# One quarter of the low parts on GpSimd, and a fourth seven-product chunk in three feed-forward parts

## The chip, the cores and the metric

The kernel runs on one core of a Trainium2 chip. The core has five engines with instruction queues of their own: TensorE (PE in the profile; its weight loads are shown as PEld), VectorE (DVE), ScalarE (ACT), GpSimd (POOL) and SyncE (SP), which only issues transfers. The metric is the device time of one launch, in microseconds (us); less is better.

## The reference

Two layers, each of them: half a feed-forward step, a mixer (self-attention of one of two kinds, and attention into a memory), half a feed-forward step. The sequence has 256 rows of 1024 values, all in 32-bit floats. A feed-forward part is

```
def swiglu(h, w_gate, w_up, w_down):          # (1024, 2816), (1024, 2816), (2816, 1024)
    return (jax.nn.silu(h @ w_gate) * (h @ w_up)) @ w_down
...
h = rmsnorm(x, ffn1_norm[i])
x = x + 0.5 * swiglu(h, ffn1_w_gate[i], ffn1_w_up[i], ffn1_w_down[i])
```

There are four such parts (two layers, two steps). They are called parts 1 to 4 here; in the code they are `(l, nm)` = (0, 1), (0, 2), (1, 1), (1, 2). The mixer of layer 1 stands between parts 3 and 4.

## The kernel before

**Split weights.** No product is a single matmul. A weight block `raw` (f32) is split into `hi`, its value rounded to fp32r by ScalarE (line 338, `split_hi`), and `lo` = `raw` - `hi`, made by VectorE (line 356, `split_lo`). The activations are split in the same way (`xh`, `xl`). Each product is then three matmuls of 512 columns into one PSUM tile: hi with xh (line 511), lo with xh (line 514), hi with xl (line 517), in `dense`.

**Chunks.** Weights come in chunks of 1 MB (128 partitions x 2048), loaded on SyncE's queue into three buffers `raw`. Each chunk has four units of 512 columns, q = 0 to 3. `hi` and `lo` have four buffers of 2048 columns each. In `dense`, TensorE waits for the low part of the unit that it needs, so all of a chunk's units are needed, but one after another. A raw buffer comes free when its splits are done, a hi and lo buffer when TensorE has used it.

**A feed-forward part.** The gate and up weights make 22 chunks (11 groups of 256 columns, two halves of the inner dimension). Eighteen are plain: two units at a time are split (`w` = 2, 1024 columns), and a chunk is used in 24 matmuls. The other four are multiplied by a scheme with seven products for eight (`pair_items`), for which VectorE forms sums of blocks (`wsum`, line 350) before they are split. The down weights make 11 chunks of 256 rows, c = 0 to 10. A plain one is split unit by unit (512 columns) and used in 24 matmuls. In parts 2 to 4 the chunks in `SEVEN`, 1, 4 and 7, are multiplied by the scheme with seven products: four sums (`wsum`), seven units to split instead of four (the last three of them in tiles called `gxh` and `gxl` for all but the first such chunk), 21 matmuls, and four sums of activation blocks (`sf`, line 681) with their own split (`h` from `hr`, lines 690 and 694) in the place of the one split of `ht` (lines 665 and 667). The last three down chunks are used together, 6 matmuls of each in turn.

**Order.** The program is written out engine by engine at build time. A planner, `Flow`, keeps an estimate of the time at which each engine will be free, and Python generators (`split_hi`, `split_lo`, `evac`, `finish`, ...) emit their next instruction when the estimate says that its inputs are there (`calm_v`: when VectorE is less than 0.4 us behind). On the chip each engine then works its own list strictly in order and waits where an input is late. The planner's estimates are not measured times, and do not know of one engine holding up another.

**GpSimd** before the change computes the rotary tables (between 120 and 200 us), reciprocal square roots by a power operation (`rsqrt`, line 532), and one of the two rotary products (line 1259).

Of the kernel before, what the change touches and what calls it, by code (L numbers as in the profile page):

```python
# [12 lines left out]
F32 = mybir.dt.float32  # L13
# [13 lines left out]
NG = FF // 256  # L27
# [15 lines left out]
SLACK = 0.4  # L43
# [99 lines left out]
def kernel(  # L143
# [10 lines left out]
    nc = tc.nc  # L154
    PSUM = bass.MemoryType.PSUM
    NRAW, NHL, NT2 = 3, 4, 19
    flow = Flow()
# [27 lines left out]
    def load_x(tb, hf, queue=None):  # L185
        (queue or nc.sync).dma_start(out=xs[tb][:, hf * 512:(hf + 1) * 512],
                                     in_=x[0, tb * P:(tb + 1) * P, hf * 512:(hf + 1) * 512])
# [53 lines left out]
    class Chunk:  # L241
        def __init__(self, parts):
            self.parts = parts
            self.raw = self.arrive = None
            self.block = [None] * 4

    class Item:
# [3 lines left out]
        def __init__(self, raws, uses=8, w=1):  # L251
            self.raws, self.uses = raws, uses
            self.hi = self.lo = None
            self.hit, self.lot, self.st = [None] * 7, [None] * 7, [None] * 4
            self.n, self.frees, self.takes, self.gives, self.guest = 1, 1, 0, 0, False
            self.sums, self.t = [], []
            self.index = len(items)
            w = 1 if len(items) < 2 else w
            self.units = [(self.own(q, w), q, w, None) for q in range(0, 4, w)]
            items.append(self)  # L260

        def own(self, q, w=1, i=0):
            return lambda: self.raws[i].raw[:, q * 512:(q + w) * 512]
# [7 lines left out]
    chunks, items = [], []  # L271
    raw_left = [NRAW]
# [6 lines left out]
    def add_raw(parts):  # L279
        chunks.append(Chunk(parts))  # L280
        return chunks[-1]

    def add_chunk(parts, uses=8, w=1):
        return Item([add_raw(parts)], uses, w)

    def loader():
        for i, c in enumerate(chunks):
            yield lambda: raw_left[0] > 0
            raw_left[0] -= 1
            c.raw = wraw.tile([P, 2048], F32, tag="raw", name=f"raw{i}")  # L290
            dma_free[0] = max(dma_free[0], flow.now)
            n = len(c.parts)
            for j, (dst, src) in enumerate(c.parts):
                nc.sync.dma_start(out=dst(c.raw), in_=src)
                dma_free[0] += 2.9 / n
                if i < 2 and j % 2:
                    for q in range((j - 1) * 4 // n, (j + 1) * 4 // n):
                        c.block[q] = dma_free[0] + LAT
                if i == 1 and j == 1:
                    load_x(1, 1)  # L300
                    dma_free[0] += 0.7
            c.arrive = dma_free[0] + LAT
            c.block = [t or c.arrive for t in c.block]
            if i == 0:
                load_x(0, 1)
                dma_free[0] += 0.7
            if i > 4 and late_done[0] < len(late_loads):
                dst, src = late_loads[late_done[0]]
                late_done[0] += 1
                nc.sync.dma_start(out=dst, in_=src)  # L310
                dma_free[0] += 0.3
# [4 lines left out]
    def calm_v(i):  # L316
        return lambda: flow.free["V"] <= flow.now + SLACK or i <= at[0] + AHEAD
# [24 lines left out]
    def split_lo():  # L342
        for i, it in enumerate(items):
            if it.sums:
                yield lambda: all(r.raw is not None for r in it.raws) and g2.left >= it.takes + 2
                yield max(r.arrive for r in it.raws)
                it.t += [g2.take([P, 512], F32, "wsum") for _ in range(it.takes)]
                for j, (x, y) in enumerate(it.sums):
                    yield calm_v(i)
                    nc.vector.tensor_sub(it.t[j], x(), y())  # L350
                    it.st[j] = flow.dve(512)
            for src, q, w, dep in it.units:
                yield lambda: it.hit[q] is not None
                yield it.hit[q]
                yield calm_v(i)
                nc.vector.tensor_sub(it.part(1, q, w), src(), it.part(0, q, w).bitcast(F32))  # L356
                t = flow.dve(512 * w)
                it.lot[q:q + w] = [t] * w
            raw_left[0] += it.frees
            g2.give(it.gives)  # L360

    def k4(t):
        return t.rearrange("p (k n) -> p k n", k=4)
# [4 lines left out]
    def cols4(w, c, c0, n, o, pieces=1):  # L368
        st = 4 // pieces
        return [((lambda raw, a=a: k4(raw)[:, a:a + st, o:o + n]),  # L370
                 w[c * 512 + a * P:c * 512 + (a + st) * P, c0:c0 + n].rearrange("(k p) n -> p k n", p=P))
                for a in range(0, 4, st)]
# [1 line left out]
    def rows2(w, r):  # L374
        return [(lambda raw: k2(raw), w[r * 256:(r + 1) * 256, :].rearrange("(k p) n -> p k n", p=P))]

    SEVEN = {(0, 1): (), (0, 2): (1, 4, 7), (1, 1): (1, 4, 7), (1, 2): (1, 4, 7)}
    PAIR = {(0, 1): 4, (0, 2): 3, (1, 1): 3, (1, 2): 3}

    def turned2(w, r):  # L380
        src = w[r * 256:(r + 1) * 256, :].rearrange("(k b i) n -> b i k n", k=2, b=4)
        return [((lambda raw, b=b: k2(raw)[b::4]), src[b]) for b in range(4)]
# [6 lines left out]
    def seven_item(it, guest):  # L389

        r = [it.own(q) for q in range(4)]
        t = lambda j: lambda: it.t[j]
        it.n, it.uses, it.takes, it.gives, it.guest = 1 if guest else 2, 7, 4, 4, guest
        it.sums = [(r[1], r[0]), (r[3], t(0)), (r[3], r[1]), (r[2], t(1))]
        it.units = [(r[0], 0, 1, None), (r[2], 1, 1, None), (r[3], 2, 1, None)] + [(t(j), 3 + j, 1, j) for j in range(4)]
# [46 lines left out]
    def plan_ffn(l, nm, wg, wu, wd):  # L442
        def parts(g, c):
            pieces = (4, 2)[len(chunks)] if len(chunks) < 2 else 1
            a = cols4(wg[l], c, g * 256, 256, 0, pieces)
            b = cols4(wu[l], c, g * 256, 256, 256, pieces)
            return [q for ab in zip(a, b) for q in ab]

        gu = {}
        pair = PAIR[l, nm]  # L450
        work = [(g, c) for g in range(NG) for c in range(2)]
        if pair is not None:
            rest = [w for w in work if w[0] not in (pair, pair + 1)]
            n = 2 * pair
            p = iter(rest[n:])
            work = rest[:n]
            loads = {}
            for x in ("11", "m1", "p", "12", "m5", "p", "22", "m7", "p", "m6", "p", "m3", "p", "p", "21", "m2", "p", "m4"):
                work.append(next(p) if x == "p" else x)
            work += list(p)  # L460
            blocks = {"11": (pair, 0), "12": (pair + 1, 0), "22": (pair + 1, 1), "21": (pair, 1)}
            raws = [Chunk(parts(*blocks[x])) for x in ("11", "12", "22", "21")]
            made, mk = pair_items(raws)
            which = dict(zip(("11", "12", "22", "21"), raws))
        for w in work:
            if w in ("11", "12", "22", "21"):
                chunks.append(which[w])
            elif isinstance(w, str):
                mk[w]()
            else:  # L470
                gu[w] = add_chunk(parts(*w), 8, 2)
        plan[l, nm, "gu"] = gu
        plan[l, nm, "work"] = [w for w in work if w not in ("11", "12", "22", "21")]
        if pair is not None:
            plan[l, nm, "pair"] = made
        dn = []
        for c in range(NG):
            dn.append(add_chunk(turned2(wd[l], c)))
            if c in SEVEN[l, nm]:
                seven_item(dn[-1], c != SEVEN[l, nm][0])  # L480
            elif c >= NG - 3:
                u = dn[-1].units
                u[1], u[2] = u[2], u[1]
        plan[l, nm, "dn"] = dn
# [133 lines left out]
    def ffn(l, nm, xt, gc_next):  # L618
        hts = [None] * NG
        htt = [None] * NG  # L620
        sv = SEVEN[l, nm]
        prog = [-1]
# [997 lines left out]
        return nxt  # L1620


    flow.spawn(loader(), idle=True)
    flow.spawn(split_hi(), idle=True)
    flow.spawn(split_lo(), idle=True)
    flow.step()
    xt = Xt(PAIR[0, 1] is not None)

# [90 lines left out]
```

## Time and profile before

| | |
|---|---|
| median of 3 runs | 955.98 us (955.21 to 956.04) |
| the profiled execution, its own time | 955.69 us |
| its span in the trace | 953.9 us |
| instructions | 13334 |
| TensorE, VectorE, ScalarE, GpSimd busy | 99%, 86%, 62%, 11% of the span |
| parts 2, 3, 4 in the trace | about 315 to 492, 492 to 668, 774 to 954 us |

A busy engine is one with an instruction in progress. Matmuls overlap in the trace: each is shown with 0.39 us, while the next one starts earlier. VectorE's instructions overlap a little too, so the price of one in a row of them is the distance between starts.

### The profile page before, as it was taken

The numbers are of one execution on the slowest core, as the hardware profiler recorded it, in microseconds if no ns is written. First come the engines' busy times: TensorE is split into PE (matmuls) and PEld (weight loads), VectorE is DVE, ScalarE is ACT, GpSimd is POOL, SyncE is SP. The second block draws the span as 40 slices with busy tenths as digits, with TensorE's granted clock in tenths as the row PEclk, the third lists the DMA queues.
The fourth block names the chain that finished last, engine by engine and source line by source line (L and its number), as shares of the span: only waits on it lengthen the run. The fifth ranks groups of instructions, "written<-read, shape, count | busy, mean of one in ns | idle before, by whom it ended". The sixth has DMA issues, their size and how long they took to land.

```text
span 953.9 us, 13334 instructions
## 1 busy us (share of the span) xinstructions
PE 945.6 (99%) x4475; PEld 774.1 (81%) x4475; DVE 820.0 (86%) x1483; ACT 587.0 (62%) x1121; POOL 109.1 (11%) x160
## 2 busy tenths in 40 slices
PE   9999999999999999999999999999999999999998
PEld 7888888887777888888888888888787778888886
DVE  7898978888777899979889899796999888999884
ACT  6556566677676746647546656564676865665650
POOL 1000057621210100000000000000434200000000
PEclk9999999999999999999999999999999999999999
DMA  8987799486525387887746679775641367588751
GB/s 265 289 263 236 224 354 296 158 276 210 177 90 177 97 266 225 262 287 219 245 146 219 208 226 288 247 253 166 196 158 57 121 214 228 183 275 276 239 197 45
DMA packets 169887, 204.04 MB, mean 214 GB/s; under 512 B 10137, under 2 KB 145114, under 8 KB 169818
## 3 DMA queue, kind: packets, MB, share of 16 engines
q1 hardware_dynamic: 169498, 202.78, 66.0%
q8 instruction: 35, 0.57, 0.3%
q10 hardware_dynamic: 320, 0.40, 0.1%
q14 instruction: 34, 0.28, 0.1%
HBM read 188.99 MB, written 14.16 MB: 213 GB/s over the span
## 4 chain that ended last, share of the span: by engine, by line
PE 90%; DVE 6%; DMA 2%; ACT 1%; issue 1%; SPq 0%; ACTq 0%; DVEq 0%
PE gu L517 13%; PE gu L514 13%; PE gu L511 13%; PE acc L511 9%; PE acc L517 9%; PE acc L514 9%; PE pair_m L511 3%; PE pair_m L514 3%; PE pair_m L517 3%; PE pj L517 2%; PE pj L511 2%; PE pj L514 2%; DVE lo L356 2%; PE S L1360 1%; DMA x<-in_x_dram 1%; PE AV L1441 1%
## 5 line engine op out<-in xcount | busy, mean ns | idle before, releaser
L338 ACT CAST hi<-raw 128x512 fp32r<-128x512 f32 (+1 forms) x467 | 336.3, 770 | 172.6 <-DMA raw<-in_ffn_w_up_dram 45.6
L356 DVE TENSOR_TENSOR lo<-raw,hi 128x512 fp32r<-128x512 f32 (+1 forms) x467 | 391.9, 875 | 35.5 <-ACT hi L338 35.4
L514 PE MATMUL gu<-lo,xh 128*128 128x512 f32 x576 | 224.7, 390 | 0.5 <-DVE lo L356 0.5
L517 PE MATMUL gu<-hi,xl 128*128 128x512 f32 x576 | 224.5, 390 | 0.4 <-DVE xl L562 0.4
L511 PE MATMUL gu<-hi,xh 128*128 128x512 f32 x576 | 224.4, 390 | 0.0
L517 PEld LDWEIGHTS gu<-hi,xl 128*128 128x128 f32 x576 | 108.1, 188 | 23.9 <-DVE xl L562 1.7
L514 PEld LDWEIGHTS gu<-lo,xh 128*128 128x128 f32 x576 | 108.1, 188 | 23.5 <-DVE lo L356 1.4
L511 PEld LDWEIGHTS gu<-hi,xh 128*128 128x128 f32 x576 | 108.2, 188 | 22.3
L517 PE MATMUL acc<-hi,ht 128*128 128x512 f32 x280 | 109.5, 391 | 0.0
L511 PE MATMUL acc<-hi,ht 128*128 128x512 f32 x280 | 109.2, 390 | 0.0
L514 PE MATMUL acc<-lo,ht 128*128 128x512 f32 x280 | 109.1, 390 | 0.0
L338 ACT CAST hi<-wsum 128x512 fp32r<-128x512 f32 x82 | 47.7, 619 | 26.5 <-DVE wsum L350 26.5
L514 PE MATMUL pj<-lo,xh 128*128 128x512 f32 x160 | 64.0, 400 | 0.0
L517 PE MATMUL pj<-hi,xl 128*128 128x512 f32 x160 | 63.8, 399 | 0.0
L511 PE MATMUL pj<-hi,xh 128*128 128x512 f32 x160 | 63.8, 399 | 0.0
L514 PEld LDWEIGHTS acc<-lo,ht 128*128 128x128 f32 x280 | 52.6, 188 | 10.9
L517 PEld LDWEIGHTS acc<-hi,ht 128*128 128x128 f32 x280 | 52.6, 188 | 10.8
L511 PEld LDWEIGHTS acc<-hi,ht 128*128 128x128 f32 x280 | 52.6, 188 | 10.7
L532 POOL TENSOR_TENSOR xr<-v,nhalf 128x1 f32<-128x1 f32 x12 | 10.3, 861 | 435.1 <-DVE v L530 435.1
L356 DVE TENSOR_TENSOR lo<-wsum,hi 128x512 fp32r<-128x512 f32 x82 | 52.8, 680 | 0.0
L633 ACT ACTIVATE sil<-gu,xr 128x256 f32<-128x256 f32 x72 | 33.7, 468 | 29.8 <-PE gu L517 29.7
L532 POOL TENSOR_TENSOR hf<-v,nhalf 128x8 f32<-128x8 f32 (+1 forms) x20 | 31.4, 1570 | 87.3 <-DVE v L530 78.9
(232 smaller groups left out, 1429.5 us busy)
## 6 DMA issues: line engine op xcount, KB each, us to landing
raw<-in_ffn_w_down_dram SPq DMA_DIRECT2D x176, 256.0 KB, 4.5
raw<-in_ffn_w_gate_dram SPq DMA_DIRECT2D x82, 512.0 KB, 4.0
raw<-in_ffn_w_up_dram SPq DMA_DIRECT2D x82, 512.0 KB, 5.4
raw<-in_w_in_dram SPq DMA_DIRECT2D x32, 512.0 KB, 4.4
hd<-hb SPq DMA_DIRECT2D x44, 256.0 KB, 4.6
hr<-hd SPq DMA_DIRECT2D x44, 256.0 KB, 4.6
raw<-in_w_out_dram SPq DMA_DIRECT2D x8, 1024.0 KB, 5.1
raw<-in_w_mem_kv_dram SPq DMA_DIRECT2D x4, 1024.0 KB, 5.3
```

Of the source, the lines that this page charges most:

```text
L338: nc.scalar.copy(out=it.part(0, q, w), in_=src())
L356: nc.vector.tensor_sub(it.part(1, q, w), src(), it.part(0, q, w).bitcast(F32))
L511: nc.tensor.matmul(out=ps, lhsT=xh, rhs=wh, start=start, stop=False)
L514: nc.tensor.matmul(out=ps, lhsT=xh, rhs=wl, start=False, stop=False)
L517: nc.tensor.matmul(out=ps, lhsT=xl, rhs=wh, start=False, stop=stop)
L532: nc.gpsimd.tensor_tensor(out=dst, in0=v[:, :n], in1=nhalf[:, :n], op=ALU.pow)
L633: nc.scalar.activation(sil, ps[tb][:, 0:256], AF.Silu, scale=xt.r[tb])
L1360: nc.tensor.matmul(out=ss[e][:, pr, :nk], lhsT=q[rows, pr, :], rhs=k[rows, pr, :], start=i == 0, stop=i == len(passes) - 1)
L1441: nc.tensor.matmul(out=av[64 * e:64 * e + 64, pr, :], lhsT=vsrc(kb, pr, e), rhs=pts[e][:, pr, kb, :], start=(kb == 0), stop=(kb == nb - 1))
```

## The change

In parts 2 to 4 every plain chunk, of gate and up as of down, is marked `other`. For these `split_lo` leaves out the last unit (q = 3), so that VectorE makes 1024 + 512 columns of a gate or up chunk, or three units of a down chunk. A new generator `split_other` makes the last unit on GpSimd, in chunk order. A raw buffer is given back when both are done. `SEVEN` is (1, 3, 5, 7) instead of (1, 4, 7) in these parts: four chunks with seven products each. Three numbers of the program follow: 75 low parts move to GpSimd (18 gate and up and 7 down chunks in each part), TensorE has 9 matmuls fewer, and 3 chunks more need the sums. The planner takes 1.7 us for a low part on GpSimd.

```diff
+        def low(self):
+            if not self.other:
+                return self.units
+            w = self.units[0][2]
+            return [u for u in self.units if u[1] + w < 4] + ([(self.own(2), 2, 1, None)] if w == 2 else [])
...
-            for src, q, w, dep in it.units:
+            for src, q, w, dep in it.low():
...
-            raw_left[0] += it.frees
+            it.open -= 1
+            if it.open == 0:
+                raw_left[0] += it.frees
...
+    def split_other():
+
+        for it in items:
+            if not it.other:
+                continue
+            yield lambda: it.hit[3] is not None
+            yield it.hit[3]
+            yield lambda: flow.free["G"] <= flow.now + SLACK
+            nc.gpsimd.tensor_sub(it.part(1, 3), it.own(3)(), it.part(0, 3).bitcast(F32))
+            it.lot[3] = flow.pool(1.7)
+            it.open -= 1
+            if it.open == 0:
+                raw_left[0] += it.frees
...
-    SEVEN = {(0, 1): (), (0, 2): (1, 4, 7), (1, 1): (1, 4, 7), (1, 2): (1, 4, 7)}
+    SEVEN = {(0, 1): (), (0, 2): (1, 3, 5, 7), (1, 1): (1, 3, 5, 7), (1, 2): (1, 3, 5, 7)}
...
+                gu[w].other = (l, nm) != (0, 1)
...
+            dn[-1].other = (l, nm) != (0, 1)
```

VectorE, part 3, gate and up chunks 110 and 111 (the number behind `lo` counts the chunks of the whole program), before:

```order
L356 TENSOR_TENSOR lo110_0_5735<-raw101_5618,hi110_0_5734 128x1024
L644 STREAM_TRANSPOSE hb_5718<-h_5747 128x2x4x32
L794 TENSOR_TENSOR gu_u_5345<-gu_u_5345,pair_m2_5731 128x512
L356 TENSOR_TENSOR lo110_0_5735<-raw101_5618,hi110_0_5734 128x1024
L667 TENSOR_TENSOR ht_5777<-hr_5705,ht_5777 128x512
L636 SCALAR_TENSOR_TENSOR h_5799<-gu_u_5345,xr_4881,sil_5791 128x256
L356 TENSOR_TENSOR lo111_0_5762<-raw102_5687,hi111_0_5761 128x1024
L644 STREAM_TRANSPOSE hb_5801<-h_5799 128x2x4x32
L356 TENSOR_TENSOR lo111_0_5762<-raw102_5687,hi111_0_5761 128x1024
```

and the same place after the change:

```order
L362 TENSOR_TENSOR lo110_0_5792<-raw101_5657,hi110_0_5791 128x1024
L661 SCALAR_TENSOR_TENSOR h_5807<-gu1_5693,xr_4916,sil_5797 128x256
L362 TENSOR_TENSOR lo110_0_5792<-raw101_5657,hi110_0_5791 128x512
L819 TENSOR_TENSOR gu_u_5402<-gu_u_5402,pair_m2_5794 128x512
L669 STREAM_TRANSPOSE hb_5778<-h_5807 128x2x4x32
L362 TENSOR_TENSOR lo111_0_5816<-raw102_5724,hi111_0_5815 128x1024
L362 TENSOR_TENSOR lo111_0_5816<-raw102_5724,hi111_0_5815 128x512
```

GpSimd's list at the same time (chunks 110 to 114 are gate and up chunks, 115 and 117 down chunks 0 and 2; chunk 116, down chunk 1, has seven products and stays on VectorE):

```order
L378 TENSOR_TENSOR lo110_0_5792<-raw101_5657,hi110_0_5791 128x512
L378 TENSOR_TENSOR lo111_0_5816<-raw102_5724,hi111_0_5815 128x512
L378 TENSOR_TENSOR lo112_0_5870<-raw103_5788,hi112_0_5869 128x512
L378 TENSOR_TENSOR lo113_0_5899<-raw104_5819,hi113_0_5898 128x512
L378 TENSOR_TENSOR lo114_0_5950<-raw105_5849,hi114_0_5949 128x512
L378 TENSOR_TENSOR lo115_0_5997<-raw106_5892,hi115_0_5996 128x512
L378 TENSOR_TENSOR lo117_0_6149<-raw108_5974,hi117_0_6148 128x512
```

The second half of a chunk's low parts is half as wide on VectorE, and each plain chunk has one row on GpSimd, where this stretch was empty.

VectorE, part 3, where down chunk 4 (number 119) is a seven-product chunk before, and down chunk 5 (number 120) a plain one:

```order
L350 TENSOR_TENSOR wsum_6181<-raw110_6104 128x512
L350 TENSOR_TENSOR wsum_6182<-raw110_6104,wsum_6181 128x512
L350 TENSOR_TENSOR wsum_6183<-raw110_6104 128x512
L350 TENSOR_TENSOR wsum_6184<-raw110_6104,wsum_6182 128x512
L356 TENSOR_TENSOR lo119_0_6200<-raw110_6104,hi119_0_6199 128x512 x3
L356 TENSOR_TENSOR lo119_0_6200<-wsum_6181,hi119_0_6199 128x512
L356 TENSOR_TENSOR gxl0_6203<-wsum_6182,gxh0_6201 128x512
L356 TENSOR_TENSOR gxl0_6203<-wsum_6183,gxh0_6201 128x512
L356 TENSOR_TENSOR gxl1_6204<-wsum_6184,gxh1_6202 128x512
L356 TENSOR_TENSOR lo120_0_6233<-raw111_6133,hi120_0_6232 128x512 x4
```

and after, the piece that ends the preparation of down chunk 5 (number 120), now with seven products:

```order
L692 TENSOR_TENSOR ht_6335<-hr_6258,ht_6335 128x512
L719 TENSOR_TENSOR h7_6316<-hr_5608,h7_6315 128x256
L719 TENSOR_TENSOR h7_6316<-hr_5608,h7_6315 128x128
L719 TENSOR_TENSOR h7_6316<-sf_6317,h7_6315 128x512
L719 TENSOR_TENSOR h7_6323<-hr_5887,h7_6322 128x256
L719 TENSOR_TENSOR h7_6323<-hr_5887,h7_6322 128x128
L719 TENSOR_TENSOR h7_6323<-sf_6324,h7_6322 128x512
L362 TENSOR_TENSOR lo120_0_6365<-raw111_6191,hi120_0_6364 128x512 x3
L362 TENSOR_TENSOR lo120_0_6365<-wsum_6288,hi120_0_6364 128x512
L362 TENSOR_TENSOR gxl0_6368<-wsum_6289,gxh0_6366 128x512
L362 TENSOR_TENSOR gxl0_6368<-wsum_6290,gxh0_6366 128x512
L362 TENSOR_TENSOR gxl1_6369<-wsum_6291,gxh1_6367 128x512
```

Ahead of this piece stand the chunk's four sums and eight sums of activations, for down chunks 5 and 7 at once; the forms of two chunks are now made between the low parts of chunks 4 and 5.

TensorE, start of the mixer of layer 1 (`pj` is the projection, `qktp` the transposes of its first rotated block `m1`), before:

```order
L514 MATMUL pj0_6748<-lo129_0_6663,xh0_6481 128x512
L517 MATMUL pj0_6748<-hi129_0_6662,xl0_6483 128x512
L511 MATMUL pj0_6748<-hi129_0_6662,xh0_6481 128x512
L514 MATMUL pj0_6748<-lo129_0_6663,xh0_6481 128x512
L517 MATMUL pj0_6748<-hi129_0_6662,xl0_6483 128x512
L525 MATMUL qktp_6800<-ident_89,m1_6771 128x128 x4
L511 MATMUL pj1_6749<-hi128_0_6627,xh1_6482 128x512
```

and after:

```order
L536 MATMUL pj0_6835<-hi129_0_6758,xh0_6559 128x512
L550 MATMUL qktp_6879<-ident_89,m1_6846 128x128 x4
L539 MATMUL pj0_6835<-lo129_0_6759,xh0_6559 128x512
L542 MATMUL pj0_6835<-hi129_0_6758,xl0_6561 128x512
L536 MATMUL pj0_6835<-hi129_0_6758,xh0_6559 128x512
L539 MATMUL pj0_6835<-lo129_0_6759,xh0_6559 128x512
L542 MATMUL pj0_6835<-hi129_0_6758,xl0_6561 128x512
```

The transposes stand five matmuls earlier than they did.

## Rows read from the trace of the kernel before

**Rows 1.** The page, busy time of each engine over the whole span.

```profile
PE 945.6 (99%) x4475; PEld 774.1 (81%) x4475; DVE 820.0 (86%) x1483; ACT 587.0 (62%) x1121; POOL 109.1 (11%) x160
```

**Rows 2.** Waits of PE: who waited for whom, us, times, longest.

```profile
PE qktp L525 <- DVE m L1266: 0.7, 2, 0.6
PE gu L514 <- DVE lo L356: 0.5, 1, 0.5
```

**Rows 3.** Busy us (count) in windows: PE, PEld, DVE, ACT, POOL; PEclk, DMA share, GB/s.

```profile
492.00:668.00 176.00, 176.00 (x786) 145.77 (x785) 155.89 (x254) 103.93 (x173) 0.86 (x1) 1.00 0.72 230
672.00:744.00 72.00, 70.52 (x375) 55.94 (x374) 67.46 (x147) 50.07 (x139) 30.53 (x26) 1.00 0.45 146
```

**Rows 4.** Timeline of PE in part 3: start us, us, instruction.

```profile
552.49 0.39 PE L514 MATMUL gu<-lo,xh 128*128 128x512 f32 x1
...
646.10 0.39 PE L511 MATMUL m<-hi,h 128*128 128x512 f32 x1
646.33 0.39 PE L514 MATMUL m<-lo,h 128*128 128x512 f32 x1
...
650.86 0.39 PE L511 MATMUL acc<-hi,ht 128*128 128x512 f32 x1
```

**Rows 5.** Timeline of DVE in part 3, equal instructions that follow each other merged.

```profile
546.57 4.63 DVE L356 TENSOR_TENSOR lo<-raw,hi 128x1024 fp32r<-128x1024 f32 x4
...
630.83 0.28 DVE L681 TENSOR_TENSOR sf<-hr 128x128 f32<-128x128 f32 x1
631.03 0.28 DVE L681 TENSOR_TENSOR sf<-hr,sf 128x128 f32<-128x128 f32 x1
...
632.56 0.62 DVE L694 TENSOR_TENSOR h<-hr,h 128x256 fp32r<-128x256 f32 x2
...
634.91 1.89 DVE L356 TENSOR_TENSOR lo<-raw,hi 128x512 fp32r<-128x512 f32 x3
...
639.12 4.93 DVE L356 TENSOR_TENSOR lo<-raw,hi 128x512 fp32r<-128x512 f32 x8
```

**Rows 6.** Two GpSimd lines: duration ns min/median/max, first and last start, form.

```profile
L1259 POOL TENSOR_TENSOR m<-qkn,ropeS x12: 725/1063/1265, 680.9 to 730.2; 128x256 f32<-128x256 f32 x12
...
L1126 POOL TENSOR_TENSOR ropew<-ropew x20: 319/333/719, 131.8 to 187.7; 128x64 f32<-128x64 f32 x20
```

**Rows 7.** Timeline of POOL in the mixer of layer 1.

```profile
680.89 2.12 POOL L1259 TENSOR_TENSOR m<-qkn,ropeS 128x256 f32<-128x256 f32 x2 [1.08 <-PE pj L517]
684.85 2.06 POOL L532 TENSOR_TENSOR hf<-v,nhalf 128x8 f32<-128x8 f32 x1 [1.83 <-DVE v L530]
688.09 2.12 POOL L1259 TENSOR_TENSOR m<-qkn,ropeS 128x256 f32<-128x256 f32 x2 [1.19 <-DVE qkn L925]
...
707.99 2.29 POOL L1259 TENSOR_TENSOR m<-qkn,ropeS 128x256 f32<-128x256 f32 x2 [1.83 <-DVE qkn L925]
```

**Rows 8.** Timeline of DVE at the same times.

```profile
681.19 1.23 DVE L1262 TENSOR_TENSOR m<-qkn,ropeC 128x512 f32<-128x512 f32 x1
...
684.60 0.17 DVE L530 TENSOR_SCALAR v<-hss 128x8 f32<-128x8 f32 x1
...
685.93 0.68 DVE L356 TENSOR_TENSOR lo<-raw,hi 128x512 fp32r<-128x512 f32 x1
...
688.39 1.22 DVE L1262 TENSOR_TENSOR m<-qkn,ropeC 128x512 f32<-128x512 f32 x1
...
708.37 0.71 DVE L530 TENSOR_SCALAR v<-oss 128x2 f32<-128x2 f32 x1
...
709.60 1.23 DVE L356 TENSOR_TENSOR lo<-raw,hi 128x512 fp32r<-128x512 f32 x1
```

**Rows 9.** Waits of DVE from 547 to 637 us: us, times, longest.

```profile
DVE ht L667 <- ACT ht L665: 2.8, 2, 1.5
DVE h L636 <- ACT sil L633: 1.7, 2, 0.9
DVE wsum L350 <- DMA raw<-in_ffn_w_down_dram: 1.7, 1, 1.7
DVE h L694 <- ACT h L690: 0.8, 1, 0.8
```

More of the change, by code (lines that the diff above doesn't have):

```diff
@@ L255, in __init__ @@
             self.n, self.frees, self.takes, self.gives, self.guest = 1, 1, 0, 0, False
-            self.sums, self.t = [], []
+            self.sums, self.t, self.other = [], [], False
             self.index = len(items)
@@ L480, in plan_ffn @@
                 seven_item(dn[-1], c != SEVEN[l, nm][0])
-            elif c >= NG - 3:
+                continue
+            dn[-1].other = (l, nm) != (0, 1)
+            if c >= NG - 3:
                 u = dn[-1].units
@@ L1620, in mixer @@
         return nxt
+    for it in items:
+        it.open = 2 if it.other else 1
     flow.spawn(loader(), idle=True)
@@ L1625 @@
     flow.spawn(split_lo(), idle=True)
+    flow.spawn(split_other(), idle=True)
     flow.step()
```

## The prediction, made before the changed kernel had run

> **What bounds the kernel now.** First the page: TensorE is busy 99% of the span, VectorE 86%, GpSimd 11% [rows 1]. Busy time alone does not say that TensorE is the bound, since overlapping matmuls hide gaps. So next the list of what TensorE waited for [rows 2]: in the whole span it waited 0.5 us for a low part of a gate or up chunk. Then the distance between matmuls: the seven-product chunk of 21 matmuls that starts at 646.10 is followed by the next chunk at 650.86 [rows 4], which is 4.76 us or 0.2267 us a matmul, with none late. In parts 2 to 4 TensorE goes from one matmul to the next without a gap. A plain chunk takes it 24 x 0.2267 = 5.44 us. The only thing to be gained there is fewer matmuls.
>
> What stands close behind is VectorE: in part 3 it is busy 155.9 of 176 us [rows 3], so 20.1 us are idle, and in the mixer of layer 1 it is busy 67.5 of 72 us while TensorE has gaps. How far VectorE is ahead is read from two places. The first low part of the plain chunk at 546.57 is done about 547.8 and first read at 552.49: a lead of 4.7 us, the thinnest in the part, behind the pair scheme. The first low part of down chunk 7 starts at 634.91, is done at 635.6 and first read at 646.33: a lead of 10.7 us [rows 4, 5]. The change is paid out of these leads.
>
> **What it removes on TensorE.** One more chunk per part with 21 matmuls instead of 24: 9 matmuls in three parts, 9 x 0.2267 = 2.04 us. TensorE has no gaps there, so all of it counts as long as the leads last.
>
> **What it moves off VectorE.** Step prices are distances between starts: a unit of 512 columns 0.60 us, from eight that take 4.93 together, of which the last is about 0.7; a unit of 1024 columns 1.14, from four in 4.63 [rows 5]. A gate or up chunk gets 1.14 - 0.60 = 0.54 us cheaper, a down chunk 0.60. Per part 18 x 0.54 + 7 x 0.60 = 13.9 us.
>
> **What it adds on VectorE.** The fourth seven-product chunk needs four sums and seven units instead of four units: 7 x 0.60 = 4.2. Its activations need four sums `sf` of 0.20 (631.03 - 630.83) and splits of 256, 128 and 512 columns (0.34, 0.20 and 0.60, by width from rows 5), for one split of 0.60: 1.3. Together 5.5 us per part. ScalarE gets some 2.5 us per part too; it is busy 103.9 of 176 us [rows 3], which covers it.
>
> **What GpSimd costs itself.** No row has a 512-column subtraction there. Its quickest two-input instructions took 319 ns for 64 columns and 725 for 256 [rows 6], 2.11 ns a column, which makes 1.27 us for 512; the slow ones wait, and with a wait for one VectorE instruction of 1.14 it is 2.4. A chunk comes every 5.44 us, so GpSimd is never the bound. The raw buffer can be freed about a microsecond later; three buffers at one chunk per 5.44 us cover that. The last unit is needed nine matmuls (gate and up) or more after the first, 2.0 us, which covers GpSimd's latency.
>
> **What GpSimd costs VectorE.** This is the disputed term. In the mixer of layer 1 GpSimd multiplies 256 columns twice in a row [rows 7], and VectorE's instructions at those times are long: 1.23 and 1.22 us where such an instruction takes 0.68, 0.71 where its like takes 0.17, and the low part at 709.60 takes 1.23 [rows 8]. Each such stretch is about 0.55 us, or 2.1 ns per GpSimd column: the VectorE instruction stood still while GpSimd read. For 512 columns that is 1.1 us if VectorE is always caught. The four stretches sum to 2.2 us over the six GpSimd instructions of the three pairs, 0.36 each, which makes 0.73 for 512; nothing at all would be the lower end where VectorE is idle. I take 1.0: nearer the upper end, since VectorE is busy 89% of these parts, mostly with instructions of the same two-input kind. Per part 25 x 1.0 = 25 us (18 to 27.5). Against it stands that the hold is not tied to GpSimd's whole instruction: during its power operation of 2.06 us from 684.85 on, VectorE's low part took its usual 0.68 [rows 7, 8].
>
> The Trainium skill (SBUF — State Buffer, Who interferes with whom) says that a VectorE instruction with two SBUF inputs and a GpSimd instruction that reads SBUF exclude each other for the whole instruction. The stretched rows agree with the exclusion; the power operation does not agree with "whole".
>
> **The sum on VectorE.** Per part -13.9 + 5.5 + 25 = +16.6 us (10 to 19) into 20.1 us of idle time. It fits, but hardly. The place matters more. Between the thin point at 547 and down chunk 7, twelve gate and up chunks (three of them in the pair scheme just before) and four down chunks have a hold h each, and the new chunk falls in it: 12(h - 0.54) + 4(h - 0.60) + 5.5 = 16h - 3.4 us more work. VectorE waited 7.0 us in this stretch for things that came late [rows 9], and a late VectorE finds them ready. So the lead at down chunk 7 becomes 10.7 + 7.0 - (16h - 3.4) = 21.1 - 16h: 5.1 us for h = 1.0, 3.5 for 1.1, 9.4 for 0.73. The last three chunks are used 6 matmuls at a time (1.36 us): chunk 8 gains 4.76 - 4.20 = 0.56, chunks 9 and 10 lose 1.8 + h - 1.36 each. That leaves 2.8 us at h = 1.0 and 1.0 at h = 1.1. At the thin point three chunks' holds take 1.4 to 1.7 us of 4.7. So I expect no wait, with 1 to 3 us to spare.
>
> **What is only moved.** The order of the mixer of layer 1 changes in some places. The transposes there waited 0.57 us for VectorE, one of the waits of rows 2, and now stand five matmuls earlier; if VectorE comes no sooner, that is up to 5 x 0.2267 = 1.1 us more. But VectorE sets the pace in that stretch and has the same work, so what TensorE loses in one place it mostly saves in the next: I take 0, with 0 to 1.1 as bounds.
>
> **The rivals.**
>
> *The leads run out (slower).* The places are down chunks 5 to 10 of each part. It decides when less than 4.2 of the 7.0 us of waiting are really saved at h = 1.0, or less than 6.0 at h = 1.1. For it speaks that things in line (the forms of two chunks before chunk 5's low parts, the transfers of `hr`) may hold VectorE further; against it that all measured leads are large. With h = 1.1 and half of the 7.0 us, the lead at the last chunk is 1.0 - 3.5 = -2.5 us per part: 7.5 - 2.0 = +5.5, 961.4 us.
>
> *GpSimd's whole instruction holds VectorE.* Then h = 1.27: 31.8 us per part, a sum of +23.4 into 20.1, 3.3 too much in each of three parts: +9.8 - 2.0, 963.8 us. The four stretches of 0.55 for instructions of 0.73 speak against it, and so does the power operation. The Trainium skill (Perfetto Trace Analysis, Optimizing Scalar/DVE Operations) warns that moving work between these two engines might not help because they share a read port; by that rule it would come out so.
>
> *The mixer gives half back.* All as forecast but the transposes wait: 953.9 + 1.1 = 955.0 us, with 0.5 to 1.7 us of it in all such places.
>
> *It doesn't do what it says.* If the fourth chunk's sums or buffers cost TensorE what they save, about 0.7 us a part, the time stays at 956. It is the first rival at its mildest.
>
> **How the numbers follow.** The profiled execution took 955.69 us, 1.79 more than its span, and is 0.3 below the median; the sum goes by the median: 955.98 - 2.04 = 953.9 us. What a measurement here can tell from no change is about 0.2%, 1.9 us, so 954.07 is the edge of "faster", and the forecast lies just inside. Chances: forecast (953.3 to 954.6) 0.47; some more gain, since waits in the mixer may also fall (below 953.3) 0.08; mixer gives back, or no gain (954.6 to 957) 0.23; leads run out 0.14, whole hold 0.08. Of the forecast some 0.32 lie below the edge: faster 0.40, same 0.38, slower 0.22. The range leaves out half of the worst cases above 960 and a little below 953.0: 953.0 to 960.0.
>
> **What would show it.** After the change the two-input instructions of VectorE that meet a GpSimd low part should take about 1.1 us longer, in the mean 1.0 per GpSimd instruction; GpSimd's low parts should take 1.3 to 2.4 us; VectorE's idle time in part 3 should fall from 20 to about 3 or 4 us; the lead at down chunk 7 should be about 5 us; the list of TensorE's waits should stay without low parts of parts 2 to 4. The prediction is wrong if TensorE waits there for `lo` or `gxl`, or if the mixer's length moves by more than a microsecond.

## The result and the profile after

The changed kernel takes 959.36 us (median of 9 runs, 957.71 to 963.97) against 955.98 before, measured beside it: a ratio of 1.0043, interval 1.0031 to 1.0056. It is slower by 3.4 us, where a gain of 2 was forecast. The time lies inside the stated range of 953.0 to 960.0 us, but only in the part of it that was kept for rivals; the forecast itself had the wrong direction. The profiled execution took 959.59 us.

Busy times of the whole span (the answer to [rows 1]):

```profile
PE 944.4 (99%) x4466; PEld 772.4 (81%) x4466; DVE 858.4 (90%) x1501; ACT 594.6 (62%) x1136; POOL 255.4 (27%) x235
```

TensorE has its 9 matmuls fewer (4466 against 4475), and the distance between two is unchanged: 0.2267 us. VectorE is busier, not less busy. GpSimd's new line, its duration in ns (shortest, median, longest):

```profile
L378 POOL TENSOR_TENSOR lo<-raw,hi x75: 1272/1412/6035, 297.0 to 938.8; 128x512 fp32r<-128x512 f32 x75
```

What TensorE waited for, over the whole span (the answer to [rows 2]):

```profile
PE qktp L550 <- DVE m L1291: 1.6, 2, 0.9
...
PE xtp L550 <- DVE x L631: 1.3, 2, 1.0
PE S L1385 <- ACT PT L1399: 1.1, 1, 1.1
...
PE gps L231 <- DMA raw<-in_ffn_w_up_dram: 0.8, 1, 0.8
PE otp L550 <- DVE of L1537: 0.7, 1, 0.7
```

The low parts on which the prediction rested (`lo`, `gxl`) are not in the list for parts 2 to 4. Instead there is `x` at line 631. That is the residual stream, which VectorE completes at the end of a part and TensorE transposes for the next; this place is called the handover below. The others are waits in the mixer of layer 1. Windows of the handover from part 2 to part 3, of part 3 and of the mixer of layer 1 (columns as in [rows 3]):

```profile
478.00:498.00 20.00, 18.56 (x88) 14.65 (x87) 18.47 (x26) 10.30 (x16) 4.64 (x4) 1.00 0.57 182
...
672.00:792.00 120.00, 115.66 (x634) 92.10 (x633) 107.50 (x221) 84.63 (x214) 41.42 (x35) 1.00 0.44 141
```
```profile
492.00:668.00 176.00, 175.89 (x785) 145.21 (x784) 168.81 (x259) 106.53 (x176) 49.48 (x26) 1.00 0.70 225
```

A window's length less PE's busy time is TensorE's idle time: 1.44 us at the handover and 4.34 in the mixer. These two numbers are followed through the experiments. The expectations further down speak of "gaps" instead, a wider count (2.4 and 19.3 us for the changed kernel in their figures), which is not to be set against idle time. Before, the two windows were these (a second profile of the kernel before):

```profile
478.00:498.00 20.00, 20.00 (x97) 16.54 (x96) 16.64 (x25) 10.05 (x16) 0.55 (x1) 1.00 0.38 117
672.00:792.00 120.00, 118.39 (x647) 94.90 (x646) 109.98 (x226) 84.97 (x213) 34.09 (x29) 1.00 0.49 153
```

No idle time at the handover, 1.61 in the mixer (2.33 in the first profile). Over the whole span TensorE's idle time is 13.4 us (a span of 957.8 less 944.4 busy) against 8.3 before (953.9 less 945.6). Of the 5.1 us more, 1.4 are at the handover, 2.0 in the mixer and 0.8 in one wait at 84 us; most of the rest lies ahead of 330 us.

**How the handover goes wrong.** GpSimd's instruction for down chunk 8 of part 2:

```profile
468.40 6.03 POOL L378 TENSOR_TENSOR lo<-raw,hi 128x512 fp32r<-128x512 f32 x1 [4.70 <-ACT hi L344]
```

VectorE at that time, equal instructions merged, in brackets the idle time before them:

```profile
467.78 1.89 DVE L362 TENSOR_TENSOR gxl<-wsum,gxh 128x512 fp32r<-128x512 f32 x3
469.59 3.69 DVE L362 TENSOR_TENSOR lo<-raw,hi 128x512 fp32r<-128x512 f32 x6
474.49 4.05 DVE L362 TENSOR_TENSOR lo<-raw,hi 128x512 fp32r<-128x512 f32 x3 [1.21 <-ACT hi L344]
478.46 0.68 DVE L739 SCALAR_TENSOR_TENSOR x<-msum,x 128x512 f32<-128x512 f32 x1
...
481.89 0.68 DVE L631 SCALAR_TENSOR_TENSOR x<-acc,x 128x512 f32<-128x512 f32 x1
482.50 1.56 DVE L739 SCALAR_TENSOR_TENSOR x<-msum,x 128x512 f32<-128x512 f32 x1
```

and TensorE:

```profile
481.38 0.39 PE L539 MATMUL acc<-lo,ht 128*128 128x512 f32 x1
482.72 0.63 PE L550 MATMUL xtp<-ident,x 128*128 128x128 f32 x4 [0.96 <-DVE x L631]
```

GpSimd begins at 468.40 and ends only at 474.43. As long as VectorE follows one two-input instruction with the next, without a gap, they take their usual 0.60 us each and GpSimd stands still; it works in VectorE's 1.21 us of idle time. Its next instructions then catch VectorE: three low parts take 4.05 us where three took 1.89 [rows 5]. The first `x` of line 631 comes at 481.89. VectorE had no wait for TensorE's sums ahead of it, so they were there; TensorE's transposes wait for VectorE. In the kernel before, VectorE came to the same `x` early and waited for TensorE:

```profile
478.46 0.69 DVE L606 SCALAR_TENSOR_TENSOR x<-acc,x 128x512 f32<-128x512 f32 x1 [1.28 <-PE acc L517]
```

### The profile page after: what moved, and what is told of

The parts are those of the page before. It is cut to its first block, busy times and chain, and to the rows that moved or that the text cites. A ratio compares the mean times of both kernels' runs of the same rounds, so it can differ in the third digit from the quotient of the medians.

```text
span 957.8 us, 13665 instructions
## 1 busy us (share of the span) xinstructions
PE 944.4 (99%) x4466; PEld 772.4 (81%) x4466; DVE 858.4 (90%) x1501; ACT 594.6 (62%) x1136; POOL 255.4 (27%) x235
## 4 chain that ended last, share of the span: by engine, by line
PE 78%; DVE 10%; DMA 7%; ACT 2%; issue 1%; SPq 1%; POOL 0%; ACTq 0%; DVEq 0%
PE gu L542 11%; PE gu L539 11%; PE gu L536 11%; PE acc L536 8%; PE acc L542 8%; PE acc L539 8%; DMA raw<-in_ffn_w_up_dram 5%; DVE lo L362 4%; PE pair_m L536 2%; PE pair_m L539 2%; PE pair_m L542 2%; PE pj L539 2%; PE pj L536 2%; PE pj L542 2%; PE m L542 1%
## 5 line engine op out<-in xcount | busy, mean ns | idle before, releaser
L378 POOL TENSOR_TENSOR lo<-raw,hi 128x512 fp32r<-128x512 f32 x75 | 145.8, 1946 | 372.1 <-ACT hi L344 277.2
L536 PE MATMUL acc<-hi,ht 128*128 128x512 f32 x256 | 100.1, 391 | 0.0
L539 PE MATMUL acc<-lo,ht 128*128 128x512 f32 x256 | 100.1, 391 | 0.0
L542 PE MATMUL acc<-hi,ht 128*128 128x512 f32 x256 | 99.9, 390 | 0.0
L344 ACT CAST hi<-wsum 128x512 fp32r<-128x512 f32 x85 | 50.5, 620 | 44.3 <-DVE wsum L356 39.9
L542 PEld LDWEIGHTS acc<-hi,ht 128*128 128x128 f32 x256 | 48.1, 188 | 9.9
L536 PEld LDWEIGHTS acc<-hi,ht 128*128 128x128 f32 x256 | 48.1, 188 | 9.9
L539 PEld LDWEIGHTS acc<-lo,ht 128*128 128x128 f32 x256 | 48.1, 188 | 9.7
L362 DVE TENSOR_TENSOR lo<-wsum,hi 128x512 fp32r<-128x512 f32 x85 | 55.3, 678 | 0.0
L356 DVE TENSOR_TENSOR wsum<-raw,wsum 128x512 f32<-128x512 f32 x56 | 44.2, 809 | 0.4
```

Source lines behind the costliest of these rows:

```text
L344: nc.scalar.copy(out=it.part(0, q, w), in_=src())
L378: nc.gpsimd.tensor_sub(it.part(1, 3), it.own(3)(), it.part(0, 3).bitcast(F32))
L536: nc.tensor.matmul(out=ps, lhsT=xh, rhs=wh, start=start, stop=False)
L539: nc.tensor.matmul(out=ps, lhsT=xh, rhs=wl, start=False, stop=False)
L542: nc.tensor.matmul(out=ps, lhsT=xl, rhs=wh, start=False, stop=stop)
```

## The experiments

All times are medians in us. Each set ran beside the kernel before on one chip (955.90, 955.94, 956.18 and 955.90 in the four sets). "Idle" is TensorE's idle time in the two windows above, from the one profile of each run; profiles of one kernel differ by up to 1.3.

| kernel | time | ratio, interval | idle, handover | idle, mixer |
|---|---|---|---|---|
| zeros | 955.61 | 0.9997 (0.9988 to 1.0006) | 0.00 | 5.09 |
| seven_only | 955.04 | 0.9986 (0.9976 to 0.9996) | 0.00 | 2.95 |
| offload_only | 957.42 | 1.0028 (1.0012 to 1.0044) | 0.00 | 2.29 |
| spare_end | 959.00 | 1.0034 (1.0022 to 1.0046) | 0.08 | 5.29 |
| z_end | 957.48 | 1.0015 (1.0004 to 1.0027) | 0.08 | 4.32 |
| z_part2 | 956.81 | 1.0010 (0.9998 to 1.0023) | 0.08 | 3.43 |
| z_part3 | 957.17 | 1.0008 (0.9998 to 1.0018) | 0.96 | 3.75 |
| five_only | 985.95 | 1.0292 (1.0266 to 1.0318) | 2.67 | 3.05 |
| after_again | 959.88 | 1.0036 (1.0025 to 1.0048) | 1.05 | 4.47 |
| z_gu | 956.46 | 1.0003 (0.9994 to 1.0012) | 1.01 | 3.55 |
| after_F1367 | 963.39 | 1.0070 (1.0054 to 1.0087) | 1.27 | 2.16 |
| seven_F1367 | 961.45 | 1.0051 (1.0034 to 1.0067) | 0.00 | 1.58 |
| after_434 | 956.31 | 1.0003 (0.9992 to 1.0014) | 1.46 | 2.56 |
| seven_434 | 954.26 | 0.9984 (0.9973 to 0.9996) | 0.00 | 1.59 |

**zeros: the holds taken away, the order kept.** GpSimd writes without reading. The low quarter of these chunks is then missing from the product.

```diff
-            nc.gpsimd.tensor_sub(it.part(1, 3), it.own(3)(), it.part(0, 3).bitcast(F32))
+            nc.gpsimd.memset(it.part(1, 3).bitcast(F32), 0.0)
```

> The changed kernel, in which each of GpSimd's 75 low parts is a fill with zeros instead of a subtraction (so the low quarter of those chunks is left out of the product). The lists of TensorE, VectorE and ScalarE are row for row those of the changed kernel; only GpSimd no longer reads two SBUF operands. Theory A (GpSimd's subtractions hold VectorE, which then comes late to the handover from part 2 to part 3 and to the mixer of layer 1): VectorE's stretched instructions vanish, the gaps of TensorE at 480 to 498 us fall from 2.4 back to about 0.4 us, and the time falls by 2 to 4 us to 955.4 to 957.5. Theory B (the new order alone costs it: transposes placed earlier than VectorE can serve them): the gaps stay, 958.5 to 959.5 us. Theory C (the fourth seven-product chunk costs it): no change either, 959 us.

Measured: 955.61 us. Without the holds 3.75 us come back, about the 3.4 that the change lost. Its page of the profile shows the same 1501 instructions of VectorE, busy 59.4 us less (799.0 against 858.4):

```profile
PE 944.3 (99%) x4466; PEld 773.1 (81%) x4466; DVE 799.0 (84%) x1501; ACT 594.5 (62%) x1136; POOL 148.6 (16%) x235
```

GpSimd and VectorE at the same place:

```profile
470.12 0.53 POOL L378 MEMSET lo<- 128x512 f32 x1 [7.00 <-issue]
472.79 0.53 POOL L378 MEMSET lo<- 128x512 f32 x1 [2.14 <-PE m L539]
```
```profile
466.73 3.69 DVE L362 TENSOR_TENSOR lo<-raw,hi 128x512 fp32r<-128x512 f32 x6
471.54 1.90 DVE L362 TENSOR_TENSOR lo<-raw,hi 128x512 fp32r<-128x512 f32 x3 [1.12 <-ACT hi L344]
473.36 0.68 DVE L739 SCALAR_TENSOR_TENSOR x<-msum,x 128x512 f32<-128x512 f32 x1
...
479.11 0.69 DVE L631 SCALAR_TENSOR_TENSOR x<-acc,x 128x512 f32<-128x512 f32 x1 [2.23 <-PE acc L542]
```

The same list of instructions. Its three low parts take 1.90 us, VectorE begins the `x` of line 739 5.1 us earlier (473.36 against 478.46) and then waits 2.23 us for TensorE's sums: that is the cover which the changed kernel used up. Of the 5.1 us, 2.9 were there before these three low parts (the six ahead of them begin at 466.73 against 469.59). The fill takes away one thing more than the hold: it needs no `hi` and no `raw`, so GpSimd also starts earlier and a raw buffer can come free earlier. What that is worth was not measured by itself; the 59.4 us on VectorE are the hold. But 955.61 isn't the 953.9 that 9 matmuls fewer should give, and the mixer's idle time stays. A second profile of it (a typical execution; the first was the slowest of eleven):

> The zero-filled kernel again, one profile. If the order of the mixer costs about 2 us by itself: TensorE idle 4 to 4.5 of the 120 us from 672 to 792, as in the changed kernel, none at the handover at 478 to 498 us, and 955 to 956.5 us. If the holds make part of the mixer's gaps: under 3.5 us idle there.

```profile
478.00:498.00 20.00, 20.00 (x98) 16.53 (x97) 16.45 (x26) 10.85 (x19) 2.36 (x4) 1.00 0.42 128
672.00:792.00 120.00, 116.19 (x634) 92.78 (x633) 105.78 (x222) 83.49 (x210) 36.76 (x35) 1.00 0.46 149
```

955.22 us, 3.81 us idle in the mixer. It waits there for what the changed kernel waits for; in its list of waits from 668 to 800 us:

```profile
PE qktp L550 <- DVE m L1291: 1.6, 2, 0.9
PE S L1385 <- ACT PT L1399: 1.1, 1, 1.1
```

The same two waits of the same size, without any hold: they come from the order. The kernel before has no wait of `S` for `PT`, and waits 0.7 or 0.0 us at `qktp` in its two profiles.

**The two halves of the change alone.** seven_only leaves every `other` False; offload_only keeps SEVEN at (1, 4, 7).

> The fourth seven-product chunk alone: VectorE makes all the low parts. Theory A: 5.5 us more on VectorE in each part go into about 20 us of idle time, TensorE saves 9 matmuls, 2.04 us: 953.5 to 954.5 us. Theory B (order): the planner writes another order here too, with early transposes in the mixer, 955 to 957 us. Theory C: the time stays at that of the changed kernel, 958.5 to 959.5 us.

> GpSimd's low parts alone (78 of them), with three seven-product chunks as before. Theory A: no matmuls saved, VectorE held about 0.84 us by each GpSimd subtraction less 0.54 to 0.60 saved, late at the part ends: 956 plus 2 to 4, 958 to 960 us. Theory B: 956 to 958 us, by the order that comes out. Theory C: 956.0 us, no difference from before.

Measured: 955.04 and 957.42. The fourth chunk alone is a gain, though of 0.9 and not 2.0 us: it too has another order in the mixer. The low parts on GpSimd alone are a loss of 1.5 us, though nothing of it is idle time in the two windows; where it lies was not found. Neither half shows idle time at the handover (0.00 and 0.00): the wait there shows only where the holds and the fourth chunk come together.

**spare_end and z_end: the last three chunks.** The one gives the low parts back to VectorE, the other fills them with zeros and keeps the order.

```diff
-            dn[-1].other = (l, nm) != (0, 1)
+            dn[-1].other = (l, nm) != (0, 1) and c < NG - 3
```

> The changed kernel with the low parts of down chunks 8, 9 and 10 of each part back on VectorE (66 stay on GpSimd). Theory A in its narrow form (what costs is a GpSimd low part that stands still for 6 us behind VectorE and then holds it just ahead of the first x of the handover): the gaps at 480 to 498 us fall from 2.4 to about 0.4 us, the time to about 957.3 us. Theory A in its wide form (VectorE is late at the end from all the holds of a part): 959 us, no change. Theory B: 958 to 960 us, by the order.

> The changed kernel, order unchanged on every engine, with only the low parts of down chunks 8, 9 and 10 of each part (9 of GpSimd's 75) made fills with zeros, which leaves these quarters out of the product. Narrow form of the hold theory (one GpSimd subtraction that stood still for 6 us holds VectorE just ahead of the handover): the gaps of TensorE at 480 to 498 us fall from 2.4 to about 0.4, time 957.0 to 957.5 us. Wide form (VectorE is late there from all the holds of part 2): gaps stay above 1.5 us, time about 959 us.

Measured: 959.00 and 957.48. In both the handover's idle time is gone (0.08), so the narrow form holds there: without 3 of part 2's 25 instructions the wait is gone. spare_end wins nothing by it. The planner writes a third order there, with a longer wait in the mixer, and four of its seven executions have a mean clock of 0.998 or less:

```profile
PE S L1385 <- ACT PT L1399: 2.2, 1, 2.2
```

**z_part2, z_part3, z_gu: zeros in some places, the order kept.** The same fill for part 2 alone, for part 3 alone, and for the gate and up chunks alone; everywhere else GpSimd subtracts.

> The same with zeros in part 2 alone (25 of 75). If each place pays for the holds of the part ahead of it: the gaps at the handover from part 2 to part 3 vanish, those of the mixer of layer 1 stay, 957.0 to 957.5 us. If the holds cost in proportion, wherever they are: a third of 3.75 us, 958.1 us.

> The same with zeros in part 3 alone (25 of 75). If VectorE carries its lateness from part 3 into the mixer of layer 1: the gaps at 480 to 498 us stay at about 2.4, those of the mixer (672 to 792 us, 19.3 in the changed kernel) fall by 1 to 1.7 us, 957.6 to 958.4 us. If the mixer's gaps come from the order alone: no change, 959.0 to 959.5 us.

> The changed kernel, order unchanged on every engine, with the low parts of the gate and up chunks (54 of GpSimd's 75) made fills with zeros, which leaves these quarters out of the product; the 21 of the down chunks stay subtractions. If every hold costs alike: 54/75 of 3.75, 2.7 us, 956.7 us. If only the holds just ahead of a part's end cost, and those of gate and up go into VectorE's idle time: gaps at 480 to 498 us as in the changed kernel, 958.4 to 959.4 us.

Measured: 956.81, 957.17 and 956.46. z_part2 clears the handover, z_part3 doesn't, z_gu doesn't (1.01): this handover pays for the holds close ahead of it. But each kernel takes back more than its place shows. z_gu recovers 3.4 of 959.88, though only 0.8 us less idle time stands in the mixer; its profile has no wait at 84 us either. Against 959.36, z_part2 and z_part3 take back 2.5 and 2.2 us, together 4.7 where zeros takes back 3.75. That the holds' costs don't simply add is possible, but with intervals of 0.9 to 1.2 us on either side of each ratio it isn't shown.

**five_only: five seven-product chunks, no GpSimd.** A try for a faster kernel, with SEVEN at (1, 2, 4, 5, 7).

> No GpSimd low parts, and five seven-product chunks (1, 2, 4, 5, 7) in parts 2 to 4: 9 matmuls fewer again than with four, 18 fewer than before, 4.08 us. VectorE has 11 us more work in each part against about 20 us of idle time. If the room lasts: 952.5 to 953.5 us (four alone gave 955.0). If VectorE's leads run out around down chunk 7, TensorE waits there for low parts and the time is 955 us or more.

Measured: 985.95. VectorE's leads are used up, TensorE waits 20 us for low parts, and its clock falls. Two windows of its handover:

```profile
480.00:486.00 6.00, 4.05 (x17) 2.72 (x15) 5.81 (x11) 3.02 (x6) 0.00 (x0) 0.99 0.88 285
486.00:492.00 6.00, 5.28 (x14) 4.11 (x14) 5.49 (x9) 1.63 (x2) 0.00 (x0) 0.50 0.79 258
```

TensorE is idle for 1.95 us in the first, and in the second has a granted clock of 0.50, which is the lower level of 1.2 GHz: 14 matmuls where 26 go into 6 us.

**The order of the mixer.** First by other chunks in part 3 (1, 3, 6, 7), which happen to give the old order there:

> The changed kernel with chunks 1, 3, 6 and 7 instead of 1, 3, 5 and 7 in part 3, which makes the planner write nearly the old order in the mixer of layer 1 (16 matmuls of 532 stand elsewhere, against 339 in the changed kernel). If the new order there costs about 1.7 us: gaps of TensorE from 672 to 792 us about 17, as before the change, and 957.5 us. If the holds make VectorE late in the mixer whatever the order: 19 us of gaps, 959 us.

> The same chunks, 1, 3, 6 and 7 in part 3 and 1, 3, 5 and 7 in parts 2 and 4, without GpSimd: the saving of 9 matmuls (2.04 us) without holds and nearly with the old order in the mixer (8 matmuls elsewhere). If holds and order are the whole of the loss: 953.5 to 954.3 us, faster than before by 0.2%, and faster than 1, 3, 5, 7 alone. If chunks 6 and 7 in a row use up VectorE's lead in part 3: TensorE waits for low parts there, 955 us or more.

Measured: 963.39 and 961.45, both slower. Two such chunks in a row use up the lead at part 3's end; TensorE waits for low parts there (3.2 us without GpSimd) and its clock falls, without GpSimd to 0.66 over the window 654 to 660 us. As a test of the order they failed, but the mixer's idle time did fall to 2.16 and 1.58. Then with three such chunks in part 3 and four in the others:

```diff
-    SEVEN = {(0, 1): (), (0, 2): (1, 3, 5, 7), (1, 1): (1, 3, 5, 7), (1, 2): (1, 3, 5, 7)}
+    SEVEN = {(0, 1): (), (0, 2): (1, 3, 5, 7), (1, 1): (1, 4, 7), (1, 2): (1, 3, 5, 7)}
```

> The changed kernel with three seven-product chunks (1, 4, 7) in part 3 and four in parts 2 and 4; GpSimd makes low parts in all three. The mixer of layer 1 then stands in the old order but for 8 matmuls; TensorE has 3 matmuls more than in the changed kernel, 0.68 us. If the new order there costs about 1.7 us: 958.3 us, with 17 us of gaps from 672 to 792 us. If only the holds cost: 960 us, with 19 us of gaps.

> The same numbers of seven-product chunks (four, three, four) without GpSimd. The mixer of layer 1 stands exactly in the old order; 6 matmuls fewer than before, 1.36 us. If the loss of four sevens alone (955.0 in place of 953.9) was the order in the mixer: 954.5 us, 17 us of gaps there. If it was a cost of the fourth chunk itself: 955.2 us.

Measured: 956.31 and 954.26. after_434 has 76 subtractions on GpSimd and 3 matmuls more than the changed kernel, and is 3.6 us faster than that kernel was in its second set (after_again):

```profile
478.00:498.00 20.00, 18.54 (x88) 14.60 (x87) 18.48 (x25) 9.90 (x16) 5.22 (x5) 1.00 0.59 186
672.00:792.00 120.00, 117.44 (x642) 93.64 (x641) 107.77 (x222) 85.40 (x216) 42.48 (x35) 1.00 0.47 150
```

The handover costs the same 1.46, the mixer 2.56 in place of 4.34. seven_434 has neither loss, and is the fastest kernel here: 1.64 us faster than before, against 1.36 worked out for 6 matmuls.

**More looks at the changed kernel and at before.** after_again, two single profiles, and one of the kernel before.

> The changed kernel unaltered, run beside the others of this set, so that they can be compared on one chip, and for a second profile. If its excess is a property of the program: 958.5 to 960 us, gaps at 480 to 498 us between 1.5 and 2.5 us. If the first measurement came out high by chance: about 957.5 us.

> The changed kernel again, one profile. If TensorE's waits at the handover from part 2 to part 3 can bring down the granted clock, an execution with a mean clock below 0.999 shows a granted clock well below 1 between 482 and 500 us, and takes 1.5 to 4 us longer; one at 1.00 shows none and takes 958 to 960 us.

> As the look before: a fall of the clock between 482 and 500 us if the mean clock is below 0.999, and 958 to 960 us without one.

> The kernel before again, one profile. If the wait at 84 us belongs to chance (when the first transfers arrive): a wait of TensorE for a transfer at 83 to 86 us appears here too in some size. If it belongs to the changed program: none, and 955 to 957 us.

Measured: 959.88, 959.34, 961.91 and 955.04. The excess is the program's own. In the second look the mean clock was 0.998, and the fall stands not at the handover, as expected, but in the mixer:

```profile
750.00:756.00 6.00, 5.14 (x32) 3.74 (x30) 4.33 (x10) 3.42 (x9) 0.00 (x0) 1.00 0.57 178
756.00:762.00 6.00, 5.74 (x27) 5.00 (x28) 4.48 (x11) 4.38 (x20) 1.07 (x1) 0.72 0.00 0
```

and in the first profile, with the same wait, it does not fall:

```profile
756.00:762.00 6.00, 6.00 (x40) 5.10 (x37) 5.64 (x16) 5.36 (x21) 2.12 (x2) 1.00 0.11 11
```

It follows the wait of `S` for `PT`, the wait that the new order brought. In all, 9 of the changed kernel's 22 executions have a mean clock of 0.998 or less, of spare_end 4 of 7, of offload_only 3 of 11, of z_end 2 of 12, of z_part2 1 of 11, of zeros, z_gu, z_part3, after_434, seven_only and seven_434 none of 68, and of before 3 of 105. In five_only and the two kernels with 1, 3, 6 and 7, where TensorE waits for low parts, all 17 have. The wait at 84 us in part 1, 0.6 to 2.0 us in the changed kernel's four profiles, shows with 0.3 in the new one of before too. It shows with 1.0 in seven_F1367 as well, which has no low part on GpSimd, so the holds are not needed for it.

## Why the prediction was wrong

**Right: what is removed, and the hold.** The 9 matmuls save 2.04 us. VectorE's instructions that met a GpSimd low part were longer by 63 us together (each against its form's usual duration), 0.84 us for each of the 75; 1.0 was taken, from [rows 7, 8]. The fill with zeros gives nearly the same: 59.4 / 75 = 0.79. The rival in which every instruction holds for its whole length (1.27) is out. GpSimd's quickest took 1.27 us, as worked out from [rows 6].

**Right: the leads.** Down chunk 7's first low part, in part 3:

```profile
643.41 1.88 DVE L362 TENSOR_TENSOR lo<-raw,hi 128x512 fp32r<-128x512 f32 x3
```
```profile
648.54 0.39 PE L539 MATMUL m<-lo,h 128*128 128x512 f32 x1
```

Done at about 644.1, read at 648.54: a lead of 4.4 us, where 5.1 was forecast. VectorE's idle time in part 3 is 7.2 us (176 less 168.81), where 3 or 4 were forecast: it is 12.9 us busier there and not 16.6, as 25 holds of 0.84 in place of 1.0 make.

**Wrong: "So I expect no wait, with 1 to 3 us to spare."** The step looked at low parts alone. Behind the last of them VectorE still owes TensorE the `x` of the next part, and the cover there was not priced: VectorE was early by 1.28 us in the trace of before, where it could be read, and by 2.23 in zeros. With the holds VectorE came 5.1 us later to the piece ahead of it. The handover from part 2 to 3 shows 1.05 to 2.19 us of idle time in the four profiles, mean 1.5; in one of the four another 0.7 stands at the end of part 3. The rival "the leads run out" had the right kind of mechanism, but at chunks 5 to 10, where none did.

**Wrong: "I take 0, with 0 to 1.1 as bounds"** for the new order in the mixer. The reason given, that VectorE sets the pace there and TensorE saves in the next place what it loses in one, failed: two of the transposes waited 1.6 us together (0.7 and 0.0 before), and a wait for ScalarE (`S` for `PT`, 1.1) came in that the prediction had not seen. Idle time there is 4.34 to 4.47 us in four profiles against 2.33 and 1.61. zeros prices the order alone, with no hold: 955.61 against 953.9, 1.7 us. The prediction's own sign, the mixer's length moving by more than a microsecond, came in. The rival "the mixer gives half back" named the place, with a third to a half of the size.

**What the two make together.** after_434 against seven_434 prices the holds in the old order of the mixer, beside a fourth chunk in parts 2 and 4: 956.31 - 954.26 = 2.05 us, with 1.46 of idle time at the handover. Order alone 1.7, these holds 2.05, saving 2.04: the sum is +1.7 us; measured were +3.4 and +3.7. So the medians leave 1.7 to 2.0 us. A part of this is the executions with a fallen clock: without them the changed kernel's median is 959.06, 0.3 to 0.8 less. Another part may be the wait at 84 us, 0.6 to 2.0 in each of the changed kernel's profiles and 0.0 and 0.3 in those of before; it stands in an unchanged part of the program, and why it is longer there is open. In the profiled execution the idle time that came with the change is placed (handover, mixer, 84 us); for the medians, what is left stays open.

## What to carry to other kernels

Work that is moved off an engine and still competes with it should be priced at each place where that engine hands over, not only at the leads of what was moved: at a part's end the cover is that engine's own wait for the other, here 1.28 us in the trace of before. A change of order by a planner is a cost of its own; it can be told from the rest by an instruction that keeps every list and drops the suspected conflict, as the fill with zeros did (which also drops the instruction's own waits for its inputs). Half of a change may be the better one: the fourth chunk without GpSimd, and only in parts 2 and 4, gives 954.26 us (0.9984, 0.9973 to 0.9996).

## What the hardware showed that was not expected

GpSimd and VectorE do not take turns. While VectorE went on without a gap with instructions of two operands, GpSimd's subtraction stood still; in 11 cases of 75 it took 3.6 to 6.04 us in place of 1.27; it came in when VectorE had a gap, and then VectorE's next instruction was the longer one (three in 4.05 us for 1.89). The Trainium skill (SBUF — State Buffer, Who interferes with whom) lets the one that starts first keep the ports for its whole instruction. The trace agrees that they exclude each other. It does not agree with the rest, as far as the profile's starts go: GpSimd's instruction of 468.40 had started, and seven of VectorE's started and ended before it did, each of them starting 0.08 us ahead of the end of the one before.

A GpSimd instruction that only writes 512 columns took 0.53 us and did not lengthen VectorE's (three low parts in 1.90 us, with the fill of 472.79 among them).

TensorE's clock fell towards its lower level after waits as short as 1.1 and 2.0 us, in some executions and not in others. It was 0.72 over 6 us in the mixer at 756 us, after a wait of 1.12 us in a stretch with other gaps, where another execution of the same program with the same wait kept 1.00. And it was 0.72 over 6 us at the wait of 2.0 us at 84 us (after_again):

```profile
84.00:90.00 6.00, 4.00 (x11) 2.85 (x11) 5.90 (x13) 2.36 (x3) 0.00 (x0) 0.72 0.92 315
```
